# Moving a covering block, the value projection and the layer norm, and a new adaLN layout, in a two-layer mLSTM and convolution kernel

## The chip, the cores and the metric

The kernel runs on one core of a Trainium2 chip, and no other core takes part. The metric is the device time of one execution in microseconds (us); lower is better. The times shown are medians of several executions, and one execution more was taken by the hardware profiler, which is where the rows of the profile come from.

## The reference, cut to what matters

Two layers (`DEPTH = 2`) of width 1024 act on 512 prompt tokens and 8 sample tokens. Cut to its data flow, a layer is:

```
mod = silu(c) @ w_ada + b_ada                     # (1024 x 3072), per sequence
shift, scale, gate = split(mod, 3)
h = rmsnorm(x, norm_w) * (1 + scale) + shift
xm, zm, ga, gb, zc, gm, gc = split(h @ w_in, 7)   # seven products of 1024 x 1024
xm_c = silu(causal_dwconv(xm, width 4))
q, k = xm_c @ w_q, xm_c @ w_k * DH**-0.5          # per head, 4 heads of 256
v = xm @ w_v                                      # per head, from xm, not from xm_c
i, f = split(concat(q, k, v) @ w_gate + b_gate)   # the gate sum: 3072 -> 8
hm, C, n, m = mlstm(q, k, v, i, log_sigmoid(f))   # stabilised, state per head
hm = (groupnorm(hm) * gn_w + skip * xm_c) * silu(zm)
u = causal_dwconv(ga * sigmoid(gb), width 31)
u = silu(layernorm(u, cln_w, cln_b)) * silu(zc)
merged = sigmoid(gm) * (hm @ w_br_m) + sigmoid(gc) * (u @ w_br_c)
x = x + gate * (merged @ w_out)
```

A last RMSNorm follows. The outputs are y and the new states of the mLSTM and of both convolutions.

## The kernel before, in words

All activations lie transposed: 8 tiles of 128 channels (`KT = 8`) by 520 columns (512 prompt columns, then 8 sample columns), worked on in two halves of 260 columns (`HALF`). Every large product is made by `dense` (L179 to L192, matmul at L188) in blocks of 128 output channels. Each weight and each input is split in a high and a low part, so a block takes 3 matmuls for each of the 8 input tiles and each half: 24 for a half, 48 for a block, all of 128x128 weights by 260 columns. `dense_pair` (L248) does two such blocks interleaved. A half's sum lies in one of three PSUM buffers of the tag "d", and must be evicted (by ACT or DVE) before the buffer is free for the third half after it. `split_w` (L163 to L177) brings the weights: a DMA on SP's queue into `raw` (two buffers), a cast on ACT to `whi` (L173), and the remainder on POOL in four quarters to `wlo` (L176).

The order in each engine's queue comes from a scheduler that simulates the program; `issue_after` pins a piece behind a given matmul. The 31-tap convolution runs on DVE, one instruction for a tap of a channel tile (L506 to L523, the taps at L515). Its pieces lie in a list, and `fill(n)` takes up to n of them where it is called.

Of the adaLN product `mod` there are six chunks of 512 outputs for a layer; chunks 0 to 3 are shift and scale, which the norm needs first, and 4 and 5 are the gate, which only the last product needs. `ada_load` brings a chunk's 2 MB, in four DMAs. `ada_mul` (L286) has one matmul for each of the 8 input tiles: the 32 columns of c (9 of them in use) as weights, 512 columns of w_ada moving; the tiles k go to four groups of 32 PSUM partitions, two tiles to a group (L292). ACT copies the 128x512 result to `asb` (L294). `tail` then has four matmuls that turn 128 columns each by a selection matrix `sel32` and so add the four groups (L300), and DVE adds the bias (L301) and makes the scale (L306). The trace has each of these float32 matmuls as two passes: 16 for a chunk, and 8 for its tail.

The order of a layer's work on PE is:

1. In layer 0, the chunks 0 to 5, with the input's norm and the first pair of blocks, `gab(0)` (ga and gb of channel tile 0), between them; in layer 1, whose chunks 0 and 1 were made in layer 0, chunks 2 to 5 at the start.
2. The loop over heads: `do_xm(h + 1)` makes the two xm blocks of the next head (ACT copies and casts them to `xm`, `xms`; DVE makes the low part, L587, and the short convolution, from which `xc` comes, L606), then `do_v(h)` projects values from `xms` (24 matmuls), then `do_qk(h)` projects q and k from the split `xc`, `xcs` (48 matmuls, eviction at L568 and L571). After the last xm comes `gab(1)` in the place of the next head's xm.
3. The gate sum: `pg` (L664, 48 matmuls as 96 passes), then a chain of small operations on ACT and DVE (L666 to L705: exp, Ln, two scans at L684 and L685, copies into `sxt` at L687 and L688), at whose end PE transposes `sxt` (`pst`, L710). PE works on `gab(2)` in the meantime.
4. The four heads of the mLSTM, with `gab(3)` to `gab(6)` and the update of the sample states (`pds`, `pqc`, `pcf`, `ppv`, `ptok`) between, then `gab(7)`.
5. zm (8 blocks), then gm and the branch product brm (16 blocks), then gc (8 blocks, sigmoid at L1035).
6. `layer_norm` (L983 to L1007), pinned behind the fourth gc block: column sums of u (`lnm`, 8 calls of `col_sums`, each 4 matmuls of 32 outputs, L195), the mean (L988), its broadcast `mb`, the subtraction on DVE (L994), the square on ACT (`lsq`, L996), the sum over channel tiles on POOL (`total`, L224), two calls of `col_sums` (`lnv`), the root by Newton steps on DVE (L155 to L160), its broadcast `lrb`, scaling on DVE (L1005), silu on ACT (L1007).
7. zc (8 blocks, silu at L1051 into `szc` tiles, of which the tag has 4 buffers that it shares with others), the product with u on DVE (L1052) and its split (L1053), then brc (8 blocks) and out (8 blocks).

## Time and profile before

| what | value |
|---|---|
| runs | 1280.69, 1283.85 and 1285.78 us, median 1283.85 |
| the profiled execution | 1279.5 us |
| its span | 1277.8 us |
| busy in the span | PE 1226.5, DVE 843.3, POOL 682.4, ACT 531.8 us |
| mean TensorE clock granted | 0.993 |
| DMA | 177.14 MB, mean 139 GB/s; the 16 engines 1.02 busy (as the profile counts it) from 10 to 40 us |

The engines are PE (matrix products; PEld is its weight load), DVE, ACT, POOL and SP (which issues DMAs). In a row of the timeline stand start and length in us, engine, line, operation, output and input, and in brackets how long the engine had been idle and what it waited for. In a row of the waits stand the waiting engine and line, what it waited for, the total in us, how often, and the longest. In a row that groups instructions stand the busy time and the mean length in ns of one. In a row of a stretch stand its limits, then for each engine the busy time and the count, then the granted clock, the busy share of the DMA engines and GB/s. Matmuls overlap: the length of one (0.28 us for 260 columns) is longer than the step from one to the next (0.12 us).

### The profile page before, as it was taken

The page shows a single profiled execution, that of the slowest core. Times are in us where ns is not written, and L with a number is a line of the kernel's source. Part 1 is how long each engine was busy: PE and PEld are TensorE (multiplying, and loading weights), DVE is VectorE, ACT ScalarE, POOL GpSimd, SP SyncE. Part 2 cuts the span into 40 slices and gives each one's busy share as a digit, 9 for nine tenths or more (in the row PEclk, how much of TensorE's full clock was granted, in tenths as well). Part 3 has the DMA queues.
Part 4 walks back from the last instruction along what each step waited for, and adds up shares of the span by engine and source line. Part 5 has one row for each costly group of instructions (what it writes and reads, how often), then busy time and mean ns, then how long its engine had stood idle before and what let it go on. Part 6 is the DMA issues. An engine that isn't in the chain of part 4 may idle for free.

```text
span 1277.8 us, 25802 instructions
## 1 busy us (share of the span) xinstructions
PE 1226.5 (96%) x10244; PEld 1155.6 (90%) x10244; DVE 843.3 (66%) x1735; ACT 531.8 (42%) x955; POOL 682.4 (53%) x899
## 2 busy tenths in 40 slices
PE   6999999999999999999999999999999999999996
PEld 3699988889999999899979997888899999989996
DVE  6495576667977993544257748666788899735424
ACT  3466554443332223532236655445434222344342
POOL 2356545556654446565635664444485545467572
PEclk9999999999999999999999999999999999999998
DMA  9632346653342342243932324566422232223322
GB/s 361 232 95 78 115 159 246 218 183 124 100 166 83 99 149 84 75 149 108 336 136 85 101 82 137 205 211 241 164 88 97 86 99 85 84 83 123 127 83 67
DMA packets 59929, 177.14 MB, mean 139 GB/s; under 512 B 13409, under 2 KB 21665, under 8 KB 55713
## 3 DMA queue, kind: packets, MB, share of 16 engines
q1 hardware_dynamic: 56928, 167.08, 38.6%
q10 hardware_dynamic: 2880, 8.42, 1.8%
q8 instruction: 80, 1.31, 0.4%
q14 instruction: 41, 0.33, 0.1%
HBM read 149.77 MB, written 25.71 MB: 137 GB/s over the span
## 4 chain that ended last, share of the span: by engine, by line
PE 80%; DVE 10%; ACT 3%; DMA 3%; POOL 2%; issue 1%; SPq 1%; DVEq 0%; ACTq 0%; POOLq 0%
PE pd L188 66%; DVE cb L780 4%; PE pds L864 3%; PE pd L248 2%; DMA o_C_p<-cf 2%; POOL wlo L176 2%; PE ada L292 1%; ACT whi L173 1%; PE pqc L768 1%; PE pcf L830 1%; DVE cv L515 1%; PE ppv L830 1%; PE pg L664 1%; DMA wada<-w_ada 1%; PE ptok L825 1%
## 5 line engine op out<-in xcount | busy, mean ns | idle before, releaser
L176 POOL TENSOR_TENSOR wlo<-raw,whi 128x256 fp32r<-128x256 f32 x680 | 523.5, 802 | 523.5 <-ACT whi L173 518.8
L188 PE MATMUL pd<-hh,whi 128*128 128x260 f32 x1728 | 495.4, 287 | 6.9 <-ACT szc L1051 5.3
L188 PE MATMUL pd<-hl,whi 128*128 128x260 f32 x1728 | 491.2, 284 | 0.0
L188 PE MATMUL pd<-hh,wlo 128*128 128x260 f32 x1728 | 490.8, 284 | 0.0
L188 PEld LDWEIGHTS pd<-hh,whi 128*128 128x128 f32 x1728 | 326.6, 189 | 14.5 <-ACT szc L1051 5.8
L188 PEld LDWEIGHTS pd<-hl,whi 128*128 128x128 f32 x1728 | 327.0, 189 | 0.4 <-issue 0.2
L188 PEld LDWEIGHTS pd<-hh,wlo 128*128 128x128 f32 x1728 | 326.8, 189 | 0.3 <-POOL wlo L176 0.2
L173 ACT CAST whi<-raw 128x1024 fp32r<-128x1024 f32 (+1 forms) x174 | 179.1, 1030 | 329.8 <-PE pd L188 276.4
L515 DVE SCALAR_TENSOR_TENSOR cv<-u,vec,cv 128x509 f32<-128x509 f32 (+6 forms) x448 | 296.5, 729 | 0.1
L780 DVE SCALAR_TENSOR_TENSOR cb<-vb,wsk,cb 128x257 f32<-128x257 f32 x128 | 72.7, 616 | 4.0 <-POOL cb L777 4.0
L188 PE MATMUL pd<-hmh,whi 128*128 128x260 f32 x256 | 72.4, 283 | 0.0
L188 PE MATMUL pd<-hml,whi 128*128 128x260 f32 x256 | 72.4, 283 | 0.0
L188 PE MATMUL pd<-hmh,wlo 128*128 128x260 f32 x256 | 72.3, 283 | 0.0
L188 PE MATMUL pd<-zl,whi 128*128 128x260 f32 x256 | 72.0, 283 | 0.0
L188 PE MATMUL pd<-zh,wlo 128*128 128x260 f32 x256 | 72.0, 283 | 0.0
L188 PE MATMUL pd<-zh,whi 128*128 128x260 f32 x256 | 71.8, 283 | 0.0
L188 PE MATMUL pd<-ml,whi 128*128 128x260 f32 x224 | 63.3, 283 | 0.0
L188 PE MATMUL pd<-mh,whi 128*128 128x260 f32 x224 | 63.3, 283 | 0.0
L188 PE MATMUL pd<-mh,wlo 128*128 128x260 f32 x224 | 63.2, 283 | 0.0
L324 DVE SCALAR_TENSOR_TENSOR xr<-pd,mod,xo 128x260 f32<-128x260 f32 (+1 forms) x32 | 15.3, 484 | 61.7 <-PE pd L188 38.9
L777 POOL TENSOR_SCALAR cb<-cb,bc 128x514 f32<-128x514 f32 x64 | 51.5, 825 | 1.3 <-PE pqc L768 1.3
L188 PE MATMUL pd<-xcs,whi 128*128 128x260 f32 x256 | 47.9, 287 | 3.0 <-ACT vv L568 2.9
(306 smaller groups left out, 2251.3 us busy)
## 6 DMA issues: line engine op xcount, KB each, us to landing
raw<-wst SPq DMA_DIRECT2D x160, 512.0 KB, 3.8
wada<-w_ada SPq DMA_DIRECT2D x36, 512.0 KB, 8.1
cb<-C SPq DMA_DIRECT2D x16, 1028.0 KB, 6.5
o_C_s<-cb SPq DMA_DIRECT2D x16, 1028.0 KB, 5.4
vb<-vsc SPq DMA_DIRECT2D x16, 514.0 KB, 5.5
wada<-w_ada ACTq DMA_DIRECT2D x12, 512.0 KB, 5.8
raw<-wqkv SPq DMA_DIRECT2D x8, 512.0 KB, 3.5
x<-x SPq DMA_DIRECT2D x4, 520.0 KB, 7.0
```

The source lines that it names most:

```text
L173: s.copy(hi, sl)
L176: g.tensor_tensor(out=lo[:, cs], in0=sl[:, cs], in1=hi.bitcast(F32)[:, cs], op=ALU.subtract)
L188: mm = te.matmul(p[:, 0:HT], a[:, ws], b[:, k, HALF[c]], start=(n == 0), stop=(n == 3 * nk - 1))
L248: te.matmul(p[:, 0:HT], a[:, ws], b[:, k, HALF[c]], start=(k == 0 and i == 0), stop=(k == KT - 1 and i == 2))
L292: te.matmul(acc[r:r + 32, :], cT[:, k, :], raw[k // 2][:, k % 2, :], start=(n < 4), stop=(n >= 4))
L324: v.scalar_tensor_tensor(out=x[:, m, c.start:c.start + n], in0=p[:, 0:n], scalar=mod[:, 16 + m, 0:1], in1=xo[:, c.start:c.start + n], op0= ...
L515: v.scalar_tensor_tensor(out=acc[a][:, sft:TP], in0=u[:, k, 0:TP - sft], scalar=wcol(sft), in1=acc[a][:, sft:TP], op0=ALU.mult, op1=ALU.add)
L664: te.matmul(pgs[n][32 * j:32 * j + 32, 0:HT], vec[:, o:o + 32], (q, kk, vv)[t][:, k, c], start=(r == 0), stop=(r == 5))
L777: g.tensor_scalar(out=cb[:, 2 * h:2 * h + 2, :], in0=cb[:, 2 * h:2 * h + 2, :], scalar1=bc[:, 0, h, b:b + 1], scalar2=1.0, op0=ALU.mult, o ...
L780: v.scalar_tensor_tensor(out=cb[:, 2 * h + j, :], in0=vb[:, h, :], scalar=wsk[:, h, j, b:b + 1], in1=cb[:, 2 * h + j, :], op0=ALU.mult, op ...
L830: te.matmul(p, a, b, start=(first and n == 0), stop=(last and n == 2))
L864: te.matmul(p[:, 0:n], kk[:, 2 * h + j, t0:t0 + 128], q[:, 2 * h + j, t0:TP], start=(j == 0), stop=(j == 1))
```

## The change

It has six parts.

1. `ada_mul` now has four matmuls for each input tile, each of 128 moving columns, and each adds its 128 outputs over all eight tiles in its own group of 32 partitions. A chunk's result is 128x128; ACT copies that, and `tail` has one transpose of it instead of four matmuls with `sel32`. There are 32 matmuls for a chunk (64 passes in place of 16).
2. The chunks 4 and 5 of layer 0 are loaded and made in its gm/brm loop, with layer 1's chunk 0 (after blocks m = 1, 3 and 5; one tile takes all three in turn). So 4 MB less are loaded at the start.
3. `do_v(h)` is issued between the two xm blocks of the next head instead of after them; the `fill(F_V)` of 10 pieces goes, and `fill(F_QK)` is ahead of `do_qk`.
4. `gab(1)` is issued after the gate sum, ahead of `gab(2)`, instead of ahead of the last value projection.
5. `layer_norm` is issued after the eighth gc block, so that it runs beside the zc blocks. POOL's sum goes: the squares of each channel tile are summed on PE, 8 calls of `col_sums` instead of 2 for a layer.
6. The silu of zc goes into tiles of three (tag "s8", three buffers) instead of the four shared ones.

```diff
@@ -43,7 +43,6 @@
-F_V = 10
 F_QK = 8
@@ -288,17 +287,17 @@
         acc = pm("ada", *ps)
         for n in range(KT):
             k = n if stream else KT - 1 - n
-            r = 32 * (k % 4)
-            te.matmul(acc[r:r + 32, :], cT[:, k, :], raw[k // 2][:, k % 2, :], start=(n < 4), stop=(n >= 4))
-        asb = t520("asb")
-        s.copy(asb[:, 0:512], acc)
+            for j in range(4):
+                mm = te.matmul(acc[32 * j:32 * j + 32, 0:128], cT[:, k, :],
+                               raw[k // 2][:, k % 2, j * 128:(j + 1) * 128], start=(n == 0), stop=(n == KT - 1))
+        asb = sml.tile([128, 128], F32, tag="asb", bufs=2, name="asb")
+        s.copy(asb, acc[:, 0:128])
 
         def tail():
             pt = pm("adat", *ps)
             ks = slice(c * 4, c * 4 + 4)
-            for i in range(4):
-                te.matmul(pt[:, i * 9:i * 9 + 9], asb[:, i * 128:(i + 1) * 128], sel32[:, 0:9], start=True, stop=True)
-            v.tensor_tensor(out=mod[:, ks, :], in0=pt[:, 0:36].rearrange("p (m r) -> p m r", r=9),
+            te.transpose(pt[:, 0:128], asb, ident)
+            v.tensor_tensor(out=mod[:, ks, :], in0=pt[:, 0:128].rearrange("p (m r) -> p m r", r=32)[:, :, 0:9],
                             in1=vec[:, O_BADA + c * 4:O_BADA + c * 4 + 4].unsqueeze(2).to_broadcast([128, 4, 9]),
                             op=ALU.add)
             if c < 4:
@@ -571,13 +570,15 @@
                                lambda c, p: s.activation(dst[:, 2 * h + m, c], p, AF.Copy, scale=sc))
             return mm if sc is not None else None
 
-        def do_xm(h):
+        def do_xm(h, between):
             ws = split_w(ap["wst"][l, PR_XM + h], 2)
             xm = s8.tile([128, 2, T], F32, tag="s4", bufs=2, name="xm")
             xms = s8.tile([128, 2, 2, T], F32R, tag="s8", bufs=S8B, name="xms")
             acs = sml.tile([128, 2, TS], F32, tag="acs", bufs=2, name="acs")
             for j in range(2):
                 k = 2 * h + j
+                if j:
+                    between()
 
                 def ev(c, p):
                     s.copy(xm[:, j, c], p)
@@ -622,26 +623,22 @@
             return proj(tuple(a[:, 512:1024] for a in w), xcs, kk, h, DH ** -0.5)
 
         gab(0, w=w01)
-        if l == 0:
-            gtails = [ada_chunk(l, adas, 4, "q"), ada_chunk(l, adas, 5, "v")]
-        else:
+        if l:
             gtails.append(ada_mul(adas, *raws.pop(0)))
-        for tail in gtails:
-            tail()
+            for tail in gtails:
+                tail()
         xc = big.tile([128, KT, T], F32, tag="xc", name="xc")
         q = big.tile([128, KT, T], F32, tag="q", name="q")
         kk = Pairs("k", F32, "kk")
         vv = Pairs("v", F32, "vv")
-        xms = {0: do_xm(0)}
+        xms = {0: do_xm(0, lambda: None)}
         for h in range(H):
             if h + 1 < H:
-                xms[h + 1] = do_xm(h + 1)
+                xms[h + 1] = do_xm(h + 1, lambda: do_v(h, xms.pop(h)))
             else:
-                gab(1)
-            fill(F_V)
-            do_v(h, xms.pop(h))
+                do_v(h, xms.pop(h))
+            fill(F_QK)
             mm = do_qk(h)
-            fill(F_QK)
         nc.sync.dma_start(ap["o_mconv_p"][l], mtail)
 
         gsb = t520("gsb")
@@ -703,6 +700,7 @@
             v.tensor_scalar(out=xe[0:4, :, hh_, S0:32], in0=sx[0:4], scalar1=ident[0:4, hh_:hh_ + 1],
                             scalar2=None, op0=ALU.mult)
 
+        gab(1, raw=True)
         mm = gab(2, raw=True)
         pt = pm("pst")
         with tc.issue_after(mm.ins):
@@ -988,17 +986,15 @@
             v.tensor_scalar(out=mean, in0=acc[:, 0:QT], scalar1=1.0 / D, scalar2=None, op0=ALU.mult)
             mb = col_bcast(mean, "mb")
             acc = pm("lnv")
-            total = s8.tile([128, T], F32, tag="s4", bufs=2, name="total")
-            for k in range(KT):
-                for c in range(2):
-                    v.tensor_tensor(out=u[:, k, HALF[c]], in0=u[:, k, HALF[c]], in1=mb[c], op=ALU.subtract)
-                sq = t520("lsq")
-                s.activation(sq, u[:, k, :], AF.Square)
-                if k < KT - 1:
-                    presum(total, sq, k == 0)
-                else:
-                    col_sums(acc, total, True, False)
-                    col_sums(acc, sq, False, True)
+            for k0 in range(0, KT, 4):
+                sqs = []
+                for k in range(k0, k0 + 4):
+                    for c in range(2):
+                        v.tensor_tensor(out=u[:, k, HALF[c]], in0=u[:, k, HALF[c]], in1=mb[c], op=ALU.subtract)
+                    sqs.append(t520("lsq"))
+                    s.activation(sqs[-1], u[:, k, :], AF.Square)
+                for n in reversed(range(4)):
+                    col_sums(acc, sqs[n], k0 + n == 3, k0 + n == 4)
             rb = col_bcast(rstd_of(acc), "lrb")
             for k in range(KT):
                 for c in range(2):
@@ -1008,8 +1004,10 @@
 
         mrg = Pairs("v", F32, "mrg")
         if l + 1 < L:
+            late = adas
             adas = ada_start(l + 1)
-            raw = ada_load(l + 1, 0, "xc")
+            turns = [(late, l, 4), (late, l, 5), (adas, l + 1, 0)]
+            raw = ada_load(*turns[0][1:], "xc")
         for m in range(KT):
             wg, wb = split_w(ap["wst"][l, PR_GMB + m], 2)
...
@@ -1021,9 +1019,13 @@
                     fill(F_GM)
 
             mm = dense(wb, hmh, hml, KT, ev)
-            if l + 1 < L and m == 3:
+            if l + 1 < L and m % 2 == 1 and turns:
+                who, _, c = turns.pop(0)
                 with tc.issue_after(mm.ins):
-                    tail = ada_mul(adas, 0, raw)
+                    tail = ada_mul(who, c, raw)
+                if turns:
+                    raw = ada_load(*turns[0][1:], "xc")
+                    tail()
 
         sgc = Pairs("k", F32, "sgc")
         if l + 1 < L:
@@ -1034,10 +1036,9 @@
             for j in range(2):
                 mm = dense(ws[j], hh, hl, KT, lambda c, p: s.activation(sgc[:, m0 + j, c], p, AF.Sigmoid))
             fill(16)
-            if m0 == 2:
-                fill(1000)
-                with tc.issue_after(mm.ins):
-                    layer_norm()
+        fill(1000)
+        with tc.issue_after(mm.ins):
+            layer_norm()
 
         if l + 1 < L:
             tail()
@@ -1047,7 +1048,9 @@
             ws = split_w(ap["wst"][l, PR_ZC + m0 // 2], 2)
             for j in range(2):
                 m = m0 + j
-                sz = t520("szc")
+                if m % 3 == 0:
+                    szs = s8.tile([128, 3, T], F32, tag="s8", bufs=S8B, name="szc")
+                sz = szs[:, m % 3, :]
                 dense(ws[j], hh, hl, KT, lambda c, p: s.activation(sz[:, c], p, AF.Silu))
                 v.tensor_tensor(out=u[:, m, :], in0=u[:, m, :], in1=sz, op=ALU.mult)
                 split_act(zh[:, m, :], zl[:, m, :], u[:, m, :])
```

Of the order that the scheduler makes, these places matter. Between `pf`, the small product behind the gate sum, and the transposes `pst` there stand 130 matmuls on PE in before and 192 in after; the matmuls of `gab(1)` are the difference. The first place to be shown is ACT's queue around the gate chain of layer 0 (a row with x stands for so many instructions that read alike). `gsb` is the copy of the gate sum, `g_1853` (in after `g_1737`) the gate values, `sg` the gb half of a gab block, and `sx` the sample part of the chain. In before:

```order
L667 COPY gsb<-pg 128x260 x2
L670 ACTIVATE g_1853<-pf,rows 48x260 x2
L533 COPY sg<-pd 128x260
L671 ACTIVATE g_1853<-g_1853 16x520
L672 ACT_TABLE_LOAD
L672 ACTIVATE g_1853<-g_1853 16x520
L173 CAST whi<-raw 128x1024
L533 COPY sg<-pd 128x260
L556 ACT_TABLE_LOAD
L556 ACTIVATE sg<-sg 128x520
L676 ACT_TABLE_LOAD
L676 ACTIVATE g_1853<-g_1853 16x520
```

In after, with the names of the new program:

```order
L669 ACT_TABLE_LOAD
L669 ACTIVATE g_1737<-g_1737 16x520
L172 CAST whi<-raw 128x1024
L532 COPY sg<-pd 128x260
L673 ACT_TABLE_LOAD
L673 ACTIVATE g_1737<-g_1737 16x520
L555 ACT_TABLE_LOAD
L555 ACTIVATE sg<-sg 128x520
L172 CAST whi<-raw 128x1024
L698 ACT_TABLE_LOAD
L698 ACTIVATE sx<-sx 16x24
L532 COPY sg<-pd 128x260
```

The gate's Ln (L676, now L673) stands ahead of the sigmoid of `sg` now, and behind the exp of `sx` (L698), which ends the chain on ACT, there stands an eviction of `gab(2)` (the last row), where before none stood within the covering block.

The second place is ACT's queue around the layer norm of layer 0: `lsq` the squares, `sgc` and `szc` evictions of gc and zc. In before:

```order
L996 ACTIVATE lsq<-u 128x520 x2
L173 CAST whi<-raw 128x1024
L996 ACTIVATE lsq<-u 128x520
L1035 ACTIVATE sgc<-pd 128x260
L996 ACTIVATE lsq<-u 128x520
L1035 ACTIVATE sgc<-pd 128x260
L173 CAST whi<-raw 128x1024
L1035 ACTIVATE sgc<-pd 128x260
L996 ACTIVATE lsq<-u 128x520 x2
L173 CAST whi<-raw 128x1024
L996 ACTIVATE lsq<-u 128x520 x2
L1051 ACT_TABLE_LOAD
```

In after:

```order
L1037 ACTIVATE sgc<-pd 128x260
L1054 ACT_TABLE_LOAD
L1054 ACTIVATE szc<-pd 128x260
L172 CAST whi<-raw 128x1024
L1054 ACTIVATE szc<-pd 128x260
L995 ACTIVATE lsq<-u 128x520 x4
L1054 ACTIVATE szc<-pd 128x260
L172 CAST whi<-raw 128x1024
L1054 ACTIVATE szc<-pd 128x260
L995 ACTIVATE lsq<-u 128x520 x4
L1054 ACTIVATE szc<-pd 128x260
```

The eight squares stood among the last gc evictions and all ahead of the first zc eviction; now they stand in two groups of four among the zc evictions.

The third is PE's queue at the start of layer 0, where `rb` is the broadcast of the norm. In before:

```order
L195 MATMUL rms<-sq,ones 32x130 x32
L292 MATMUL ada<-wada,cT 32x512 x8
L203 MATMUL rb<-yi,ident 128x130 x4
L300 MATMUL adat<-sel_83,asb 128x9 x4
L292 MATMUL ada<-wada,cT 32x512 x2
L248 MATMUL pd<-hh,whi 128x260 x2
L292 MATMUL ada<-wada,cT 32x512 x2
```

In after:

```order
L194 MATMUL rms<-sq,ones 32x130 x32
L291 MATMUL ada<-wada,cT 32x128 x32
L202 MATMUL rb<-yi,ident 128x130 x4
L299 MATMUL adat<-ident,asb 128x128
L291 MATMUL ada<-wada,cT 32x128 x8
L247 MATMUL pd<-hh,whi 128x260 x2
L291 MATMUL ada<-wada,cT 32x128 x8
```

Where two matmuls of a chunk stood there stand eight, of a quarter of the columns, and where four of a tail stood there stands one.

## The prediction

> **What bounds the kernel now.** I read the page's busy times first, then the waits of PE, then the chain that ended last.
>
> ```profile
> span 1277.8 us, 25802 instructions
> PE 1226.5 (96%) x10244; PEld 1155.6 (90%) x10244; DVE 843.3 (66%) x1735; ACT 531.8 (42%) x955; POOL 682.4 (53%) x899
> ```
>
> PE is busy for 1226.5 us of 1277.8, the next engine for 843.3. Some 51 us are idle on PE, the input's load at the start among them. All that a change can win is in those 51 us, in PE work that goes, or in PE work that gets cheaper.
>
> ```profile
> PE rms L195 <- ACT sq L216: 8.1, 4, 5.6
> PE pst L710 <- DVE sxt L688: 5.9, 2, 3.0
> PE pd L188 <- ACT szc L1051: 5.3, 2, 2.7
> PE pd L188 <- ACT vv L568: 2.9, 3, 1.0
> PE pd L188 <- ACT xms L584: 2.8, 6, 1.8
> ```
>
> These are PE's waits (total, times, longest). The first is the start, which the change leaves. The second is the end of the gate chain, the third PE without a free PSUM buffer in zc, the last two the q/k and v projections. The chain of waits agrees: most of it is PE at dense blocks.
>
> ```profile
> 528.98 120.35 PE pd L188 x1000
> 403.72 1.85 PE ada L292 x16
> 27.62 1.01 PE adat L300 x8
> 477.48 1.69 PE lnm L195 x56
> ```
>
> A thousand block matmuls in a row took 120.35 us: 0.120 us each, 5.8 for a block of 48. A chunk took 1.85, its tail 1.01, and 56 passes of column sums 1.69, which is 0.030 each.
>
> **The change part by part.** Everything is set against the profiled execution, 1279.5 us, which lies 4.4 below the median of 1283.85; I add that at the end.
>
> *The new chunks.* Nothing before has exactly their form, but the first row below comes near: 32 columns of weights in a column group, 128 rows, 130 moving columns.
>
> ```profile
> L195 PE MATMUL lnm<-u,ones 128*32 128x130 f32 x128 | 4.4, 277 | 0.0
> L195 PEld LDWEIGHTS lnm<-u,ones 128*32 128x32 f32 x128 | 3.3, 109 | 0.6
> L292 PE MATMUL ada<-wada,cT 128*32 128x512 f32 x192 | 31.0, 613 | 1.2 <-DMA wada<-w_ada 1.2
> L300 PE MATMUL adat<-sel,asb 128*128 128x9 f32 x96 | 11.9, 252 | 0.7 <-ACT asb L294 0.7
> L825 PE MATMUL ptok<-ident,kk 128*128 128x128 f32 x64 | 8.3, 272 | 0.0
> ```
>
> 128 such passes occupy 4.4 us although their weight loads last 109 ns each: four groups run beside each other. At 0.030 the 64 passes of a new chunk are 1.93 us against 1.85, and one transpose, two passes at 8.3/64 = 0.13, is 0.26 at most; I take 0.2, since it is issued among blocks. A chunk with its tail goes from about 2.85 to 2.13: 0.7 less. That, twelve times, would be 8.5 if each lay alone on PE. They don't, so I go by place.
>
> ```profile
> 28.60:52.30 23.70, 10.10 (x48) 1.00 0.82 303
> 28.60:52.30 23.70, 10.60 (x72) 1.00 0.82 303
> 46.12 0.51 PE L248 MATMUL pd<-hh,whi 128*128 128x260 f32 x2 [1.35 <-ACT hh L433]
> 57.53 1.92 PE L292 MATMUL ada<-wada,cT 128*32 128x512 f32 x16
> 59.38 1.06 PE L300 MATMUL adat<-sel,asb 128*128 128x9 f32 x8
> wada<-w_ada SPq DMA_DIRECT2D x24, 512.0 KB, 9.0
> ```
>
> These are the stretch from 28.60 to 52.30 (the chunks alone, then `gab(0)` alone), a wait in it, chunk 5 and two tails behind it, and the loads (how many, KB each, median us to landing). The stretch holds 48 passes, three chunks, 10.1 us by reason of short groups, and 72 matmuls of `gab(0)`, 10.6. Chunk 4 leaves it (10.1/3 = 3.4), its other two go from 6.7 to perhaps 4.5 as the tails shrink too (2 by 0.8). That is 3.4 + 2.2 + 1.6 = 7.2, and I let 1.0 of it be lost to waits as that of 1.35: −6.2, between −2.8 (the chunks' load and the norm set the end) and −9.6 (the short groups become as dense as `lnm`). Chunks 0 and 1 ahead of it: −1.0, of at most −1.4. Chunk 5 and two tails leave this place for good: 59.38 − 57.53 = 1.85, and 1.01 for each tail, less some overlap: −3.7. What left comes back in gm/brm, among dense blocks: two chunks and tails, 2 by 2.13, and some 0.4 for four turns between small and large matmuls, +4.7. Their loads wait on SP's queue for the chunk before, and the next `raw` stands behind that wait; but its block is due four blocks of 5.8 later, so 23 us hide it. Without that cover a load of 9 us would show. In layer 1, chunks 0 and 1 lie among blocks: −1.4. Its chunks 2 to 5 lie beside the norm:
>
> ```profile
> 655.16 1.92 PE L292 MATMUL ada<-wada,cT 128*32 128x512 f32 x16
> 657.46 1.13 PE L203 MATMUL rb<-yi,ident 128*128 128x130 f32 x8 [0.38 <-DVE yi L160]
> ```
>
> PE waits for DVE's root there, so a faster chunk ahead of it wins nothing: −1.2, of 0 to −2.8. Sum: −1.0 − 6.2 − 3.7 + 4.7 − 1.4 − 1.2 = **−8.8** (−4 to −13).
>
> *The second covering block.* The wait of 3.0 in each layer, and what follows it:
>
> ```profile
> 177.96 1.04 PE L710 MATMUL pst<-ident,sxt 128*128 128x128 f32 x4 [2.98 <-DVE sxt L688]
> 797.06 0.63 PE L710 MATMUL pst<-ident,sxt 128*128 128x128 f32 x4 [2.95 <-DVE sxt L688]
> 170.00:180.00 10.00, 7.02 (x63) 6.10 (x61) 9.19 (x21) 3.17 (x4) 5.52 (x4) 0.90 0.20 66
> 800.27 0.42 PE L188 MATMUL pd<-hh,wlo 128*128 128x260 f32 x1
> ...
> 802.44 0.39 PE L188 MATMUL pd<-hh,whi 128*128 128x260 f32 x1
> ```
>
> After each, PE runs for a while at a lower granted clock: 0.90 in the stretch at 170, and in layer 1 eleven block matmuls from 800.27 to 802.44, a step of 0.217 instead of 0.120, so 1.1 us. In layer 0 the four transposes, the `pvt` and two `ptok` cost about 0.85 more than the same in layer 1 (1.04 against 0.63 shows it). Together 2.98 + 0.85 + 2.95 + 1.1 = 7.9. Now 62 more matmuls, 7.4 us, cover the chain. It needs 2.98 more than before, so 4.4 are left over. What could hold PE: ACT's exp of `sx` waits for DVE at the chain's end, and an eviction of `gab(2)` is queued behind it on ACT; with three buffers PE can go on for two halves more, 48 by 0.120 = 5.8, before it needs that buffer. Also the new `gab(1)` gives DVE two products more ahead of the scans. I take **−7.5** (−4 to −8). The block that left the v projection is charged below.
>
> The Trainium skill ("TensorE: Matmul & The Clock Gate", Part 1) says that the clock falls after an idle window of about 3.4 us. By that alone these waits would not lower it; without the 0.85 and the 1.1 here and the 1.6 below the gain would be 3.5 us smaller and the median 1265.5. The trace shows the low clock right behind waits under 3 us, so I keep them.
>
> *The layer norm.* PE waits in zc for a buffer, because the first zc eviction stands behind all eight squares on ACT, and `szc` waits for the POOL sums that hold the tiles:
>
> ```profile
> 515.16 0.39 PE L188 MATMUL pd<-hh,whi 128*128 128x260 f32 x1 [2.67 <-ACT szc L1051]
> 1131.42 0.39 PE L188 MATMUL pd<-hh,whi 128*128 128x260 f32 x1 [2.67 <-ACT szc L1051]
> 510.00:520.00 10.00, 7.33 (x50) 6.98 (x52) 0.00 (x0) 4.22 (x8) 5.68 (x7) 0.83 0.20 70
> ```
>
> Two waits of 2.67, and a clock of 0.83 in layer 0's stretch: 1.7 us of ten, of which I count 1.6. The POOL sums go, and the zc tiles are their own, so both waits should end: −6.9. PE pays 24 matmuls more for a layer, 48 passes, 96 in all: at 0.030, +2.9, and 0.4 for turns. Sum **−3.6** (−7 if the passes hide in a stall that I don't see; +3 if a wait as long stays in each layer). Moved with it is the end of the norm, 4 blocks later. What is late then is DVE:
>
> ```profile
> 490.89 0.29 DVE L988 TENSOR_SCALAR mean<-lnm 128x130 f32<-128x130 f32 x1 [5.72 <-PE lnm L195]
> 405.58 46.02 PE pd L188 x384
> L515 DVE SCALAR_TENSOR_TENSOR cv<-u,vec,cv 128x509 f32<-128x509 f32 x16 | 11.9, 742 | 0.0
> L1005 DVE SCALAR_TENSOR_TENSOR u<-u,vec,lrb 128x260 f32<-128x260 f32 x32 | 12.8, 479 | 4.4 <-PE lrb L203 4.4
> ```
>
> DVE stood idle 5.7 us before the mean, so the convolution was done by 485.2, 33.6 after gm/brm ended at 451.6 (405.58 + 46.02). Some 17 taps more than before stand behind the branch product (17 by 0.7 = 12), so it now ends 45.6 after the start of gc; the last `lnm` comes some 51.5 after (8 by 5.8 for gc, 1.9 for a chunk, the rest `lnm` and the zc matmuls between): 6 us of slack. From `mb` to `lrb` PE has 153 zc matmuls, 18 us, and behind `lrb` 194, 23 us. Of this DVE and ACT use 6.4 for the scaling (the last row, half for each layer) and a similar time for the products, so brc should not wait.
>
> *The value projection.* It now has a block of xm between itself and what it reads, so the waits for `xms` shrink; and no weight cast stands any more between ACT's small wait for the short convolution and the evictions:
>
> ```profile
> 104.26 0.49 ACT L606 ACTIVATE xc<-acs,vec 128x8 f32<-128x8 f32 x2 [0.96 <-DVE acs L604]
> 106.01 0.51 PE L188 MATMUL pd<-xcs,whi 128*128 128x260 f32 x2 [0.96 <-ACT vv L568]
> 106.01 16.02 PE pd L188 x131
> 130.30 1.15 DVE L618 TENSOR_TENSOR xcs<-xc,xcs 128x520 fp32r<-128x520 f32 x1 [0.70 <-ACT xcs L617]
> ```
>
> 2.9 and 2.8 are at stake, 5.7, but some of the `xms` waits belong to the first projection and to slots that stay, and the last head has lost `gab(1)` as its cover between xm and q/k: the split `xcs` of its second tile was ready 131.45 − 122.03 = 9.4 us after the xm blocks ended, and PE now has 72 matmuls of the projections to bridge that, 8.6 us at 0.120 and some more where PE waits anyway. I take **−2** (−4 to +2).
>
> Sum: −8.8 − 7.5 − 3.6 − 2.0 = −21.9, so 1257.6 for the profiled execution, and with the 4.4 to the median **1262.0**.
>
> **The rivals.** *R1, the weight loads go one after the other (slower).* If the new chunk's loads of 32 columns could not go beside running matmuls, its 64 passes would cost 0.109 each as in the row of `lnm`'s loads: 7.0 instead of 1.9, 5.1 more by 12 = +61, so about 1323. The change loses from 0.059 us a pass on (21.9/768 = 0.029 above the 0.030). Against it: `lnm` has the same loads and took 0.034 a pass over all. For it: there the weights are one constant throughout, here they change with each input tile, and the moving columns come from a tile that a DMA has just filled.
> The Trainium skill ("TensorE: Matmul & The Clock Gate", Part 3) states that a weight load overlaps running matmuls only where its row group differs, and here all four share it. By that rule this rival would hold; the `lnm` row, with shared rows too, speaks against it.
>
> *R2, the convolution is late.* If the taps at 0.74 eat the 6 us, the norm ends late and brc waits: with 10 us in one layer or 5 in each, 1272. For it: DVE is the second engine and 12 us of taps came later. Chance 0.12.
>
> *R3, the gate wait stays.* The exp of `sx` holds the eviction, PE stops in `gab(2)` instead of after it, and the clock falls as before: −7.5 is not won, 1269.5. It decides where the chain ends over 4.4 later than it does now, and `gab(1)`'s two products on DVE and its sigmoid on ACT are what I can find for it. Chance 0.15.
>
> *R4, the start is bound elsewhere.* From 10 to 40 us the DMA engines are full and the norm's chain is on DVE; then of the 6.2 + 3.7 only the 3.7 is won: 1268.2. Chance 0.15.
>
> *R5, more is won.* Chunks and tails are busy for 31.0 + 11.9 = 42.9 us, twelve new ones at 2.13 would be 25.6; were the chunks at their far end, −13, the gate's waits gone whole, −7.9, and layer norm and projections at −5 and −3, the sum is −29: 1255. Chance 0.10.
>
> **How the numbers follow.** Forecast 0.45, R1 0.03, R2 0.12, R3 0.15, R4 0.15, R5 0.10. About 0.5% (6.4 us) is what a measurement of this kernel tells from no change; the three runs differ by 0.4%. All but R1, and R2 together with R3 or R4, lie below 1277.4: faster 0.93, same 0.04, slower 0.03. The range takes in R5 with some more and R2 with little over: 1252 to 1273.
>
> **What would show it.** Right: no row `pst` from DVE over 0.5 us in PE's waits, no `szc` row over 1, the granted clock near 1.00 in both stretches, 768 `ada` passes at under 0.035 each, and the stretch that ended at 52.3 ending near 45. Wrong: an `ada` group over 3 us for 64 passes (R1); `zl` or `lrb` ahead of `pd` in the waits (R2); `pd` waiting for `sg` in `gab(2)` (R3); that stretch ending near 51 (R4).

## The result, and the profile after

The changed kernel took 1271.63 us (median of 4 runs, 1267.62 to 1272.94) against 1284.82 before (4 runs): a ratio of 0.990, 95% interval 0.9875 to 0.9926. It is faster, by 13 us with 10 to 16 in the interval. The forecast was 1262.0, 22 less, with a range of 1252 to 1273. The direction and the range held; 9 us of the gain did not come. The profiled execution took 1267.62 us, 11.9 less than that of before.

The head of the page after:

```profile
span 1265.9 us, 26935 instructions
PE 1215.2 (96%) x10832; PEld 1161.1 (92%) x10832; DVE 847.2 (67%) x1735; ACT 530.1 (42%) x959; POOL 662.6 (52%) x885
```

PE is busy for 11 us less and the span is 12 shorter, so what it stood idle is the same: some 51 us. PE's waits (waiting line, what it waited for, total, times, longest):

```profile
PE rms L194 <- ACT sq L215: 7.6, 4, 5.8
...
PE ada L291 <- DMA wada<-w_ada: 3.5, 3, 2.7
PE ptok L823 <- DVE stT L710: 3.4, 2, 1.7
PE pd L187 <- ACT xms L585: 3.3, 6, 2.3
...
PE pds L862 <- DVE dd L868: 2.5, 2, 1.3
PE pds L862 <- ACT dd L865: 2.0, 3, 1.1
...
PE pd L187 <- ACT kk L570: 1.5, 2, 0.8
PE pqc L766 <- DVE dd L868: 0.9, 2, 0.4
```

The rows for `sxt` (5.9) and `szc` (5.3) are gone, as forecast. New are `stT`, `dd` and `pqc`, 3.4 + 2.5 + 2.0 + 0.9 = 8.8 us: PE now waits a few microseconds further on, in the first head of the mLSTM (7.7 of the 8.8; one wait of 1.1 for `dd` is in layer 0's second head). Before, these rows held 0.4 (`dd`), and nothing in the first head.

Where the time went shows best by the starts of stages, the first instruction of a kind on its engine in each trace (us from the start of the span):

| stage begins with | before | after | after − before |
|---|---|---|---|
| layer 0: gate sum (`pg`) | 152.9 | 130.5 | −22.4 |
| transposes (`pst`) | 178.0 | 160.3 | −17.7 |
| first zm eviction | 316.9 | 307.4 | −9.6 |
| first gm eviction | 362.3 | 352.4 | −9.9 |
| first gc eviction | 455.4 | 449.8 | −5.6 |
| first brc eviction | 563.6 | 554.3 | −9.3 |
| layer 1: gate sum | 772.0 | 751.2 | −20.9 |
| first zm eviction | 937.6 | 926.4 | −11.2 |
| first gc eviction | 1073.5 | 1062.3 | −11.2 |
| first brc eviction | 1177.4 | 1164.9 | −12.6 |
| last `frb` | 1270.4 | 1258.6 | −11.8 |

Before, `gab(1)` stood ahead of the gate sum; its 96 matmuls are 11.5 us at 0.120. Less these, the way to layer 0's gate sum is 10.9 shorter, and the way from there to zm 1.3 longer (12.8 lost, 11.5 of it the moved block) where 3.8 less had been forecast. Of the 8.2 us that layer 0 takes longer from `pst` to zm, 4.1 are work that changed its place: `gab(1)` has 96 matmuls, but only 62 more stand ahead of `pst` than before, so 34 block matmuls of the next block, once ahead of it, now come behind it (541 from `pst` to zm against 507). gm and brm pay 4.3 for the late chunks, gc and zc win 3.7. In layer 1 the stage from the end of layer 0 to the gate sum wins nothing, that from the gate sum to zm 1.8, the layer norm 1.4.

The chunks and column sums in the groups of instructions:

```profile
L291 PE MATMUL ada<-wada,cT 128*32 128x128 f32 x768 | 26.4, 284 | 3.6 <-DMA wada<-w_ada 3.5
L291 PEld LDWEIGHTS ada<-wada,cT 128*32 128x32 f32 x768 | 20.8, 113 | 7.0 <-issue 3.2 <-DMA wada<-w_ada 2.3
L194 PE MATMUL lnv<-lsq,ones 128*32 128x130 f32 x128 | 4.4, 277 | 0.0
L299 PE MATMUL adat<-ident,asb 128*128 128x128 f32 x12 | 3.5, 291 | 0.8 <-ACT asb L294 0.7
```

The end of `gab(0)` and a late chunk in the chain of waits (start, length, what):

```profile
45.49 0.97 PE pd L247 x8
...
371.07 1.88 PE ada L291 x64
```

A pass costs 26.4/768 = 0.034, a chunk 1.88, a tail 3.5/12 = 0.29. `gab(0)` ends at 46.5 where the stretch had ended at 52.3; 45 was forecast. The new layer norm's second sum is 128 passes in 4.4 us, 0.034 each.

DVE ahead of the mean in layer 0:

```profile
492.32 0.68 DVE L522 TENSOR_TENSOR u<-cv,co 128x511 f32<-128x511 f32 x1
498.94 0.29 DVE L986 TENSOR_SCALAR mean<-lnm 128x130 f32<-128x130 f32 x1 [5.94 <-PE lnm L194]
```

The convolution ends at 493.0 and DVE then waits 5.94 us for PE: the 6 us of slack that the prediction worked out.

The new waits, on PE and then on the three engines that feed it. PE at layer 0's first head:

```profile
160.29 0.60 PE L708 MATMUL pst<-ident,sxt 128*128 128x128 f32 x4
...
166.37 0.66 PE L823 MATMUL ptok<-ident,vv 128*128 128x128 f32 x4 [1.68 <-DVE stT L710]
...
178.54 1.13 PE L862 MATMUL pds<-q,kk 128*128 128x256 f32 x4 [1.26 <-DVE dd L868]
```

DVE at the same time:

```profile
161.45 1.39 DVE L514 SCALAR_TENSOR_TENSOR cv<-u,vec,cv 128x506 f32<-128x506 f32 x2
162.75 0.42 DVE L539 TENSOR_TENSOR u<-pd,sg 128x260 f32<-128x260 f32 x1
163.09 2.68 DVE L514 SCALAR_TENSOR_TENSOR cv<-u,vec,cv 128x504 f32<-128x504 f32 x4
165.68 0.42 DVE L539 TENSOR_TENSOR u<-pd,sg 128x260 f32<-128x260 f32 x1
166.02 0.29 DVE L710 COPY stT<-pst 128x144 f32<-128x144 f32 x1
```

ACT at the same time:

```profile
163.13 1.05 ACT L172 CAST whi<-raw 128x1024 fp32r<-128x1024 f32 x1 [4.24 <-DMA raw<-wst]
164.20 1.28 ACT L712 ACT_TABLE_LOAD   x1
166.35 0.22 ACT L712 ACTIVATE en<-stT 128x16 f32<-128x16 f32 x1 [0.86 <-DVE stT L710]
167.06 1.08 ACT L845 CAST v1h<-ptok 128x512 fp32r<-128x512 f32 x2 [0.50 <-PE ptok L823]
```

And the issues on SP's queue that this cast waits for:

```profile
157.99 0.34 SPq L486 DMA_DIRECT2D us<-conv  x1
158.43 0.37 SPq L166 DMA_DIRECT2D raw<-wst  x1
```

The transposes are done at 160.9, but DVE copies them to `stT` only at 166.02. It is busy with taps of the convolution (L514): the trace has 26 taps between `pst` and the first `pcf` of each layer, where before had none (there 19 ran between the gate sum and `pst`). They are those of channel tile 1: `gab(1)` now comes a stage later, and its taps come later with it. ACT stands at the same time before a cast whose raw tile was issued at 158.43, behind the load of the sample convolution, and which starts at 163.13; `en` and the values `v1h` are queued behind that cast.

In the kernel before, DVE had taps in the gate sum and the gate chain behind it:

```profile
151.58 13.49 DVE L515 SCALAR_TENSOR_TENSOR cv<-u,vec,cv 128x503 f32<-128x503 f32 x21
```

In the changed kernel it is idle there, for 14.13 us in layer 0 until the gate values come from ACT at 142.97.

### The profile page after: what moved, and what is told of

The parts are those of the page before. It is cut to its first block, busy times and chain, and to the rows that moved or that the text cites. A ratio compares the mean times of both kernels' runs of the same rounds, so it can differ in the third digit from the quotient of the medians.

```text
span 1265.9 us, 26935 instructions
## 1 busy us (share of the span) xinstructions
PE 1215.2 (96%) x10832; PEld 1161.1 (92%) x10832; DVE 847.2 (67%) x1735; ACT 530.1 (42%) x959; POOL 662.6 (52%) x885
## 4 chain that ended last, share of the span: by engine, by line
PE 76%; DVE 13%; issue 3%; ACT 3%; DMA 3%; POOL 1%; SPq 0%; DVEq 0%; ACTq 0%; POOLq 0%
PE pd L187 65%; DVE cb L778 4%; DVE cv L514 3%; PE pds L862 2%; PE pcf L828 2%; ACT whi L172 1%; DMA o_C_p<-cf 1%; PE ada L291 1%; PE pd L247 1%; PE pqc L766 1%; PE pg L661 1%; POOL wlo L175 1%; DMA wada<-w_ada 1%; DVE ac L594 1%; DVE bst L795 1%
## 5 line engine op out<-in xcount | busy, mean ns | idle before, releaser
L514 DVE SCALAR_TENSOR_TENSOR cv<-u,vec,cv 128x509 f32<-128x509 f32 (+9 forms) x448 | 298.7, 732 | 0.1
```

What stands on the lines that cost most here:

```text
L514: v.scalar_tensor_tensor(out=acc[a][:, sft:TP], in0=u[:, k, 0:TP - sft], scalar=wcol(sft), in1=acc[a][:, sft:TP], op0=ALU.mult, op1=ALU.add)
```

## The experiments

Twelve kernels were run, each timed beside the kernel before. "Profile" means the start of the last `frb` in the trace of the one profiled execution: 1270.4 in before, 1258.6 in the changed kernel. The executions of one kernel lie 1 to 11 us apart, so a few microseconds between two profiles count for little by themselves. Ratios are against before, timed in the same set of runs.

**The taps out of the way.** Tile 1 is left unconvolved here, and the other tiles' taps are held until zm:

```diff
-                filler.extend(conv31_tasks(k))
+                if k != 1:
+                    filler.extend(conv31_tasks(k))
...
-                v.tensor_tensor(out=xc[:, m, :], in0=xc[:, m, :], in1=sz, op=ALU.mult)
+                i = v.tensor_tensor(out=xc[:, m, :], in0=xc[:, m, :], in1=sz, op=ALU.mult)
...
-                fill(F_Z if m < KT - 1 else F_ZL)
+                with tc.issue_after(i.ins):
+                    fill(F_Z if m < KT - 1 else F_ZL)
```

> The changed kernel without the 31-tap convolution of channel tile 1 in both layers (that tile of u stays unconvolved), and with the other tiles' taps held until zm, so that no tap is left between the gate sum and zm. The changed kernel has 26 taps between the transposes of the gate chain and the first pcf of each layer. Theory 1 (those taps hold DVE, and with it stT, v1l and dd, for which PE waits): PE's waits for stT and dd, 3.4 + 2.5 + 2.0 + 0.9 = 8.8 us in all, fall under 1.5, the way from the transposes to the first zm eviction, 147.1 us in layer 0, becomes some 4 us shorter in each layer, and the whole some 8 us shorter, about 1263 against 1271.6. Rival 2 (PE only comes earlier to a chain whose length is set by its own latencies): the waits stay near 8.8 and the time within 2 us of the changed kernel. Nothing else should be shorter: the convolution was not what ended last in the later stages, where DVE stood idle for 5.9 us before the mean.

Measured: 1265.65 us, ratio 0.9863 (0.9847 to 0.988), profile 1255.3. The waits for `stT` go, and in their place PE waits 2.8 and 2.2 us for `v1l`, where the waits for `stT` and `dd` in the first head had been 3.8 and 3.9 in all; from `pst` to the first zm eviction it is 146.3 us instead of 147.1 in layer 0. PE's wait:

```profile
PE pu L859 <- DVE v1l L847: 5.0, 2, 2.8
```

ACT in layer 0:

```profile
166.97 1.05 ACT L172 CAST whi<-raw 128x1024 fp32r<-128x1024 f32 x1 [7.82 <-DMA raw<-wst]
168.04 1.28 ACT L713 ACT_TABLE_LOAD   x1
169.33 0.22 ACT L713 ACTIVATE en<-stT 128x16 f32<-128x16 f32 x1
169.45 1.06 ACT L846 CAST v1h<-ptok 128x512 fp32r<-128x512 f32 x2
```

SP's queue:

```profile
159.65 0.37 SPq L758 DMA_DIRECT2D cb<-C  x1
160.12 0.84 SPq L166 DMA_DIRECT2D raw<-wst  x2
```

`stT` was ready at 161.5 here, and `en` still ran at 169.33: ACT waits 7.82 us for the raw tile, with `en` and `v1h` behind it. Theory 1 falls as stated, for the waits don't fall under 1.5; theory 3 was formed from this. But the run changed two things. With the taps gone the 1 MB load `cb`, which in the changed kernel was issued behind the tile (159.45), is issued ahead of it, and the cast runs 6.4 us after `pst` instead of 2.8. That is 3.6 later, and in layer 1 3.5 by the same count, more than the 2.8 and 2.2 that PE waits: by this estimate a tile as early as in the changed kernel would have left no wait.

**The taps kept, but held until zm** (the second half of the edit above):

> The changed kernel with all of its taps kept, but those that the list gives out in the zm loop held until the product of xc in that zm block, so that tile 1's 28 taps of a layer run in zm and later instead of beside head 0. Theory 1: the waits for stT and dd go as in the kernel without these taps (some 8 us less up to zm, both layers together), and 28 taps of 0.73, 20 us a layer, come on top of DVE's work from zm to gc, where it had 37 us idle in 190 by the stretches; the 5.9 us ahead of the mean are used up, and up to 4 us a layer come back as a wait of PE in zc. Time between 1262 and 1268. Rival 2: waits for stT and dd stay at 8.8, time 1271 to 1276.

Measured: 1269.39 us, ratio 0.9891 (0.9875 to 0.9906), profile 1260.1. The wait for `v1l` is 4.2 here too, and the later stages cost nothing: from the first zm eviction to layer 0's last norm it is 333.0 us against 332.6. So the taps fit in zm and behind it, but moving them alone wins nothing that can be told, and the time is above the 1262 to 1268 expected: here too `cb` is ahead of the tile on SP, and the cast waits 7.16 us for it.

**`gab(1)` back ahead of the last value projection:**

```diff
             else:
+                gab(1)
                 do_v(h, xms.pop(h))
...
-        gab(1, raw=True)
         mm = gab(2, raw=True)
```

> The changed kernel with its fourth part undone: gab(1) is issued again ahead of the last value projection, and gab(2) alone covers the gate chain. Theory 1 (the part moved the wait and did not remove it): the wait for sxt comes back with about 3 us a layer and some lower clock, 6 to 8 in all, the waits for stT and dd, 8.8, go, and the time is within 3 us of the changed kernel's 1271.6. Rival 2: as the chain behind the transposes is bound by its latency, undoing the part loses the 7.5 us of the prediction: about 1279. Rival 3 (the move won what was forecast and the loss is elsewhere): also about 1279.

Measured: 1266.96 us, ratio 0.9885 (0.9862 to 0.9908), profile 1256.5: no slower than the changed kernel, and 2 us faster in the profile. The old wait is back, and in the first head none of the new ones is left (one of 1.9 for `dd` is in the second):

```profile
PE pst L708 <- DVE sxt L686: 4.6, 2, 2.3
```

So the fourth part moved the wait and did not remove it. The forecast of 7.5 us for it, and the rivals 2 and 3 with it, fall.

**Two covering blocks, but the next two,** `gab(2)` and `gab(3)`, with `gab(1)` where it was:

```diff
-        gab(1, raw=True)
-        mm = gab(2, raw=True)
+        gab(2, raw=True)
+        mm = gab(3, raw=True)
...
-            nxt = gab_b(h + 3, True)
+            nxt = gab_b(h + 4, True)
...
-        mm = gab(7)
```

> The changed kernel with gab(1) ahead of the last value projection, as in the kernel before, and gab(2) and gab(3) as the two covering blocks; the heads take gab(4) to gab(7), and no block is left behind them. So tile 1's taps fill DVE's idle time during the gate chain again, and none is beside head 0. Theory 1: both the wait for sxt (under 0.5) and the waits for stT and dd (under 2) are gone, so 8 us less up to the heads' end, 1264; against that the end of the heads has lost gab(7) as cover for the last normalisations, of unknown cost, 0 to 6 us. Time 1262 to 1270. Rival 2: the waits for stT and dd stay at 8.8 as PE comes as early as in the changed kernel: 1271 or more.

Measured: 1275.01 us, ratio 0.9938 (0.9919 to 0.9957). The wait for `sxt` is gone, and in the first head there is none of the new ones (2.0 for `dd` come in later heads). From the gate sum to `pst` it is 29.4 us against 29.8 in the changed kernel, so PE came as early, and no tap runs there: the chain's own length is not what made the waits, and rival 2 falls. But the end of the heads lost its cover, and the time is above the 1262 to 1270 expected:

```profile
PE pth L918 <- POOL q L812: 8.0, 2, 4.0
```

Its profiled execution took 1281.87 us, 6.9 above the median, so its rows serve for the waits alone.

**The sample convolution later,** so that one load less stands ahead of the raw tile on SP:

```diff
+                if k in (1, 2):
+                    waiting.append(samples)
+                else:
+                    samples()
...
             nxt = gab_b(h + 3, True)
+            while waiting:
+                waiting.pop(0)()
```

> The changed kernel with the sample part of the convolution of tiles 1 and 2 written behind the blocks of head 0 instead of at the end of their gab blocks, which takes one load (us) out of SP's queue ahead of the weights of gab(3); the taps stay where they are. Theory 3 (two things reach the values of head 0 late at the same time: DVE, held by the taps, with stT at 166.0 us, and ACT, whose cast waits 4.2 us for a raw tile that SP issues behind the sample convolution's DMAs, with en and v1h queued behind it, until 164.2; taking either away alone leaves the other): ACT's wait for raw in that place falls from 4.2 to under 2, the waits of PE stay, and the way from the transposes to the first zm eviction in layer 0 stays within 1.5 us of 147.1. Theory 1 (only the taps): no change at all. Rival 4 (only the load): 3 to 4 us less in each layer.

Measured: 1278.78 us, ratio 0.998 (0.996 to 1.0). ACT in layer 0:

```profile
160.43 1.05 ACT L172 CAST whi<-raw 128x1024 fp32r<-128x1024 f32 x1 [1.50 <-PE pd L187]
...
166.85 0.22 ACT L719 ACTIVATE en<-stT 128x16 f32<-128x16 f32 x1 [4.07 <-DVE stT L717]
```

The cast is at 160.43 instead of 163.13 and doesn't wait for its DMA any more, and `en` runs no sooner: now it waits 4.07 us for DVE's `stT`, and PE 1.9 in each layer. So DVE's lateness alone holds PE in the first head. The way from `pst` to zm was not 147 but 153.8, against the expectation: between the first `pds` and zm this kernel loses 7 to 9 us a layer. In the second head, behind the place where the moved pieces now stand, PE has new waits, 6 us of them in layer 0 and 4 in layer 1: 2.4 for `dd`, 2.3 for `wsl`, and

```profile
PE pds L869 <- DVE v1l L853: 4.8, 2, 3.3
```

What makes DVE late there was not taken apart.

**Both at once:**

> Both at once: the late sample convolution and the taps held until zm. Theory 3: neither DVE nor ACT is late now; PE's waits for stT, dd and v1l (8.8 us in the changed kernel, 5.0 for v1l in the one without these taps) fall under 2 in all; the way from the transposes to zm in layer 0 falls from 147.1 to 143 to 144, some 3 us a layer; the later stages cost nothing, as they did not with the taps in zm. Time 1264 to 1267 against 1271.6. Theory 1 would give the same as with the taps in zm alone, 1269 and a wait of 4 to 5 us for v1l.

Measured: 1266.05 us, ratio 0.9875 (0.9842 to 0.9909), profile 1257.1. The scores start 7.3 us after `pst` instead of 13.2, but zm begins little sooner (145.8 against 147.1). There are 4.4 us of waits for `v1l`: 2.7 in the second head, where the moved pieces stand, and 1.7 in the first (0.7 and 1.0 in the two layers). So the expectation missed. The waits of the first head have a reason that ACT shows:

```profile
164.81 1.05 ACT L172 CAST whi<-raw 128x1024 fp32r<-128x1024 f32 x1 [4.78 <-DMA raw<-wst]
```

With the taps gone from there the 1 MB load `cb` came ahead of the raw tile on SP, at 157.78, and the cast ran at 164.81.

**The first two parts alone,** then **the first alone,** on the kernel before (the hunks of `ada_mul`, and for both parts those of `turns` and `gtails`, of the diff of the change):

> The kernel before with the first two parts of the change alone: the new chunks (four matmuls of 128 columns, one transpose) and layer 0's chunks 4 and 5 in the gm/brm loop. The prediction's first term gave -8.8. By the starts of the stages the changed kernel had won 10.9 us up to the gate sum, some of it from the projections, and lost 4.3 in gm/brm. Expected: 7 to 9 us less than before, 1274 to 1276. Rival (the win ahead of the gate sum comes from the new place of the value projections): 2 to 4 us less. Rival (the weight loads of the new chunks go one after the other): slower.

> The kernel before with the first part alone: the new chunks and the single transpose, with layer 0's chunks 4 and 5 still loaded and made at the start. With both parts the profile was 7.3 us shorter than the kernel before. If the work on PE sets the start, the layout alone wins the 0.7 a chunk of the prediction, 8.5 in all by the sum and some 6 to 8 in the profile. If the load of the 12 MB sets it, the six chunks of the start win little and only layer 1's count: 2 to 4 less, and the second part (4 MB later) is what wins the rest. Expected: 3 less, 1279 to 1281.

Measured: 1272.73 us, ratio 0.9925 (0.9898 to 0.9952), profile 1263.1 (−7.3) for both parts; 1274.85 us, ratio 0.9949 (0.993 to 0.9967), profile 1265.3 (−5.1) for the layout. By the profiles the chunks bring 5.1 and their new place 2.2; by the times it is 6.5 and 3.1, with 2 to 4 us of uncertainty. That is what the prediction's first term described. The layout's gain is nearer the case in which PE's work sets the start (6 to 8 expected) than the one in which the load does (2 to 4), but this does not settle it.

**The layer norm as before:**

> The changed kernel with the layer norm as before: pinned behind the fourth gc block, squares summed on POOL, zc's silu into the four shared tiles. The prediction gave this part -3.6; by the stages the changed kernel won 3.0 us from gc to brc in layer 0 (without the second chunk of layer 1) and 1.4 in layer 1. Expected: 3 to 5 us slower than the changed kernel, 1275 to 1277, with PE's wait for szc back at two times 2.7. Rival (what it wins as waits it pays back as 96 passes more): within 1.5 us of 1271.6.

Measured: 1294.13 us, ratio 1.0093 (1.0057 to 1.0128): slower than the kernel before. PE's wait:

```profile
PE pd L187 <- ACT szc L1055: 17.0, 2, 8.8
```

Here the old wait of two times 2.7 is two times 8.5. The convolution ends at 496.1 in this kernel, 43 us after the first gc eviction (452.9); before it was at 485.2, 30 after (455.4). So the norm, wherever it is issued, begins near the end of gc, and its squares and POOL sums then stand ahead of zc's evictions in full. The expectation (3 to 5 us) missed because it took the part by itself. What more it cost than these waits was not taken apart.

**The value projection as before:**

```diff
-                xms[h + 1] = do_xm(h + 1, lambda: do_v(h, xms.pop(h)))
-            else:
-                do_v(h, xms.pop(h))
+                xms[h + 1] = do_xm(h + 1, lambda: None)
+            do_v(h, xms.pop(h))
```

> The changed kernel with its third part undone: the value projection again behind both xm blocks of the next head (no fill ahead of it). The prediction gave the part -2. By the stages of the two profiles the way from the first value projection to the gate sum, less the blocks that moved, is the same within 0.6 us in layer 0. Expected: within 2.5 us of the changed kernel, so the term was nought; 2 or more slower would bear the prediction out.

Measured: 1266.96 us, ratio 0.988 (0.9862 to 0.9898), profile 1257.9, 0.8 less than the changed kernel.

**The third and fourth parts both undone:**

> The changed kernel with its third and fourth parts undone: only the chunks, their new place, and the layer norm are left of the change. If the parts 3 and 4 won the 9.5 us of the prediction, this is 9 us slower than the changed kernel, 1281. By the runs so far they won nothing net: 1266 to 1271, with PE's wait for sxt back at 4.6 to 6, none over 1 us for stT or v1l, and the wait for szc gone.

Measured: 1266.33 us, ratio 0.9878 (0.986 to 0.9896), profile 1259.2, 0.6 more than the changed kernel. The two parts together won nothing that the times can tell.

**The values ahead of the weight cast on ACT,** with the taps held until zm:

```diff
-            s.copy(hi, sl)
+            if after is not None and i:
+                with tc.issue_after(after):
+                    s.copy(hi, sl)
+            else:
+                s.copy(hi, sl)
...
-            nxt = gab_b(h + 3, True)
+            nxt = gab_b(h + 3, True, after=cp if h == 0 else None)
```

Here `cp` is the second cast of head 0's values.

> The changed kernel with the taps held until zm, and with the cast of gab(3)'s second weight tile put behind the casts of head 0's values on ACT. Theory 3: what is left of the wait without the taps, 4 to 5 us for v1l, is ACT standing in front of a raw tile that has not landed; with the casts of the values ahead of it that wait falls under 1.5 in all, and head 0's scores start 3 to 4 us sooner after the transposes than in the changed kernel (13.2 us there). The time falls only if the next exp on ACT does not meet the same raw tile: 1263 to 1269. Rival 2 (latencies of PE's own chain): the wait for v1l stays.

Measured: 1265.06 us (1261.33 to 1267.54), ratio 0.9863 (0.9838 to 0.9887), profile 1252.3, 6.3 less than the changed kernel. ACT in layer 0:

```profile
161.50 0.22 ACT L716 ACTIVATE en<-stT 128x16 f32<-128x16 f32 x1 [2.01 <-DVE stT L714]
164.19 1.08 ACT L849 CAST v1h<-ptok 128x512 fp32r<-128x512 f32 x2 [2.47 <-PE ptok L827]
165.15 1.06 ACT L174 CAST whi<-raw 128x1024 fp32r<-128x1024 f32 x1
```

No wait of PE for `stT` or `v1l` is left; 1.0 for `dd` is, in later heads, and 1.5 for `qc` is new. The scores start 8.0 us after `pst`, 5.2 sooner than in the changed kernel. Of the kernels that compute everything this is the fastest, in the profile by 4 us, though its profiled execution was the fastest of its four and the next ratio is 0.9875. By the times its interval overlaps those of the changed kernel and of the three with parts 3 or 4 undone, so how much it beats them by is open.

## Why the prediction was right, and where it was not

Followed from run to run, the profile gives −7.3 for the chunks and their place (the run with these alone), −3.9 for the layer norm (from there to the run without parts 3 and 4) and −0.6 for parts 3 and 4 (from there to the changed kernel); that these make −11.8 in all is so by construction, and each is a difference of single executions. By the ratios the same steps are −9.6, −6.0 and +2.8, each with some 4 us of uncertainty either way. The prediction had −8.8, −3.6 and −9.5. On both counts the first two terms hold and the third does not.

That the range held is in part luck: the time lies 1.4 us inside its upper end, which was set for a late convolution (R2, 1272), and the convolution was not late. The direction is not luck; the chunks and the layer norm carried it.

**The chunks** were right: 0.034 a pass against 0.030, 1.88 a chunk against 1.93, 0.29 a tail against 0.2, +4.3 against +4.7 in gm and brm, the start near 46.5 against 45. Rival R1 is out. The rule of the Trainium skill ("TensorE: Matmul & The Clock Gate", Part 3), that a weight load overlaps only where row groups differ, does not hold for these loads: all four share the rows, each load lasts 0.113 us, and the passes come every 0.034. Rival R4 is out too: the start was won.

**The layer norm** was right in its mechanism, its slack of DVE included (5.94 against 6), and in its size as far as the times tell. What the prediction missed is that the part is needed: with the taps as late as the change makes them, the norm in its old form costs two waits of 8.5.

**The gate stall** is the step that failed: "Now 62 more matmuls, 7.4 us, cover the chain", taken at −7.5. The matmuls did cover it, and the wait for `sxt` went. But the step asked only what could hold PE ahead of the transposes. Of `gab(1)` it moved the matmuls and two products, and not the 31 pieces of convolution and the DMAs of the sample part that follow from it. In the kernel before 19 of those taps ran in the gate chain, in time in which DVE now waits (14.13 us in layer 0); now 26 run in the first head, where `stT` and `dd` are due, and the next weight tile is late on SP's queue at the same time. Rival R3 had the price (7.5 lost, 1269.5) by another mechanism: PE has no wait for `sg`.

The runs show that DVE's lateness alone is enough to hold PE (3.9 us for `stT` in the first heads with the tile early). That the tile alone does so is shown only for a tile some 3.5 us later than in the changed kernel (5.0 us for `v1l` without the taps); whether it held PE in the changed kernel itself is open, and the estimate above speaks against it. It matters for a remedy, because with the taps out of the way the tile comes later. With DVE free and ACT's order changed the waits are gone, and from `pst` to zm it is 4.0 and 2.6 us less in the two layers than in the changed kernel. The 7.5 was forecast against `gab(1)` in its old place: against that run the way from the gate sum to zm, less the 11.5 of the moved block, is 2.9 and 2.3 shorter, so 5.2 of the 7.5 can be had this way. In the whole time the two kernels' intervals overlap.

The signs named for a right forecast all came: no row `pst`, no row `szc`, a clock of 1.00 in both stretches, passes at 0.034, a start that ends at 46.5 where 45 was named. They looked only at the waits that were to go, so none of them could show the ones that came.

**The value projection** (−2) can't be told from nothing. In the profile it is −2.7 with `gab(1)` in its old place (1259.2 to 1256.5) and +0.8 with it moved (1257.9 to 1258.6), but the first compares the slowest of four executions with the fastest of four; by the ratios the two steps are +0.9 and +2.6, each with some 4 us of uncertainty. Its range was −4 to +2.

**The chances.** Faster had 0.93. The likeliest case, with 0.45, was not what came; R2's time was nearest (1272) without its mechanism, and R3's term was the one that was lost, without its mechanism. The three rivals on the short side had been priced one at a time.

## What to carry to other kernels

When a block is moved, list everything that it sets free, not its own instructions alone: here 31 filler pieces for DVE and three DMAs on an in-order queue came later with it and landed where the next chain was due. A wait that is covered with other work can come back at the next place where the same engines are late; look one stage further than the wait that goes, and name a sign there. And price the parts of a change together where one takes the cover of another: the old layer norm cost 5 us of waits in the old order and 17 in the new.

## What was not expected of the hardware

The lower clock came at a new place. Before, the first 28.6 us had it at 1.00; after a wait of 2.71 us for a chunk's load the changed kernel shows this (stretch, busy times, clock, DMA share, GB/s), and block matmuls 0.42 us long:

```profile
0.00:28.60 28.60, 17.13 (x258) 12.37 (x258) 19.74 (x58) 11.17 (x20) 8.27 (x18) 0.94 0.94 361
```

```profile
19.93 0.64 PE L291 MATMUL ada<-wada,cT 128*32 128x128 f32 x16 [2.71 <-DMA wada<-w_ada]
...
22.51 0.42 PE L247 MATMUL pd<-hh,wlo 128*128 128x260 f32 x1
```

So this start, faster on PE, waits longer for its loads (3.5 us for `wada` in the waits, 1.2 before) and pays some of it back in clock. With the layout alone the same stretch had 0.88. Together with the three of before, the low clock followed waits of 2.7 to 3.0 us, shorter than the 3.4 that the Trainium skill ("TensorE: Matmul & The Clock Gate", Part 1) gives; it did not follow every one of them. Over all runs the length alone does not decide it: after a wait of 2.32 us (the run with `gab(1)` back, at 785.7) the next 5 us had 0.66, and after one of 2.98 (the values first, at 682.4) they had 1.00.

A 512 KB weight tile took 4.7 us from its issue to the cast that waited for it (158.43 to 163.13), and 6.9 when a 1 MB load had been issued 0.5 us ahead of it (160.12 to 166.97, without the taps; 6.5 with both pieces late, 158.33 to 164.81).
